# A hybrid recurrence and convolution layer: the launch's scheduler orders the instructions by its timeline model

## The chip, the cores and the metric

The kernel runs on one core of one Trainium2 chip. The metric is the device time of one execution in microseconds (us); a value given for a kernel is the median over its runs. A profile is one further execution that the hardware profiler recorded, with a time of its own. The engines are PE (matrix products; PEld is its weight load), DVE (vector), ACT (scalar and activations), POOL, and SP, which here only issues DMA.

## The reference

One layer over a sequence of 2048 tokens of width 1024, with a context of 256 tokens:

```
shift, scale, gate = split(silu(c) @ w_ada + b_ada, 3)      # the same with c_ctx for the context
h  = rmsnorm(x, norm_w) * (1 + scale) + shift
p  = h @ w_in                                               # 1024 x 9216
q, v, zf, zb = four of the five column groups of p, 8 heads of 128 each
f  = lb + (1 - lb) * sigmoid(z)                             # forward and backward; k = 1 - f
S_t = diag(f_t) S_{t-1} + k_t v_t^T ;  o_t = S_t^T q_t      # in both directions, started from the context's states
y_hg = rmsnorm(o) * silu(gate columns)
y_cv = b * conv3(c * h) * silu(gate)                        # within rows of 64 tokens, four more column groups
out  = rmsnorm(x + gate * (concat(y_hg, y_cv) @ w_out), final_norm_w)
```

All is float32 in the reference.

## The kernel before, in words

**Products.** A float32 operand is split into two float16 parts, and each product takes three matmuls (high by high, high by low, low by high; lines 839 to 841). On top of that the input and the output projection use a seven-product scheme for 2x2 blocks (`seven`, from line 830) instead of eight, for which sums and differences of blocks of weights and tokens are formed first. These operands are named B11, T1, T2, B21, T3, B22, T4 on the token side; they are prepared once per group of 512 tokens and stored in DRAM (Hd).

**Stages in the program.** (1) The start, lines 1238 to 1264: the first 512 tokens (x, four tiles of 128x1024) are loaded, squared on ACT (L220) and normalised on DVE (L225); a pair of weight tiles is loaded (L333, `load_pair`); then `modulate` (from L177) loads the modulation matrix in sixteen tiles `wa` of 512 KB (L182) into four buffers (the tags f and K, two each) and multiplies it (`pada`, L184), with the transposes of the first tokens and a second pair of weights between its steps. Only after `modulate` does the program load the context's two tiles (`xt_c`) and the second token group's four tiles (printed as `x` in the profile) at L1259. The context's tiles use the tag Q of six buffers, the second group's four tiles are set aside in the pool `hp`. `modulate_end` and `affine` make scale and shift of `pada`, and the first products follow (`plain`, L1346 to L1348). (2) Eight heads in four segments of 512 tokens each, 32 windows: in each, the products for gates, values and queries of one segment go beside the scan of the segment before (`scan_steps`, L636). The scan is a chain: a diagonal product (`Ad`, L528), five levels (`A`, L554) in each of which PE multiplies, DVE updates K and Q (L414, L421), ACT copies (`km`, L537), then two more levels (L568, L578), the transposes of K, the states (L602) and the output (`o`, L658 and L659). The tiles f and K that carry it have two buffers. (3) Short convolutions, 18 windows. At their first, pools are closed and others opened, and large operands C are loaded back (L900). (4) The output projection, from about 1800 us of the profile on.

**What sets the order of the work.** Two things. First the program: in each window, `run` (L1294) emits the products, and between them, by weights in a table PACE (L45), the steps of the scan and of other preparations. Second the launcher's scheduler. When the tile context of line 1520 is closed, it walks the traced program in a simulated machine: an engine (or SP, which issues DMA) that is free there gets the earliest instruction of the program whose inputs are finished, and whose buffer has come free, at that simulated moment. So an instruction can be passed by later ones. The order that comes out is fixed; semaphores are then put in for it, and on the chip each engine takes its instructions strictly in that order and waits where one isn't ready. Which physical buffer a tile gets is set in the same walk.

The context's constructor has a switch for the simulated machine. Without it, the scheduler uses its default model of what instructions and transfers take.

## Time and profile before

| | us |
|---|---|
| median of 3 runs | 2226.85 |
| lowest and highest | 2223.29, 2228.72 |
| the profiled execution, its own time | 2224.16 |
| its span from first to last instruction | 2222.2 |

| engine | busy us | share of the span |
|---|---|---|
| PE | 2113.2 | 95% |
| DVE | 1659.9 | 75% |
| ACT | 1158.3 | 52% |
| POOL | 112.5 | 5% |

In the profile, `out<-in` names the tile written and the tiles read, `x8` counts instructions in a row or a group, and `[0.20 <-DMA wa]` at the end of a row says that the engine had been idle for 0.20 us and what ended this. In the table of windows each row is a stretch of the span: its length, then the busy time of PE, PEld, DVE, ACT and POOL with the number of instructions in parentheses, the granted PE clock (1.00 is full), the mean busy share of the 16 DMA engines, and GB/s. In the groups, the figures behind the bar are busy us and mean ns of one, then idle time before them. In a table of waits they are us in total, number of times, and the longest. SPq marks SP's queue: the rows of it are issues of DMA, not the transfers.

### The profile page before, as it was taken

What the parts mean: (1) busy time and instruction counts of PE and PEld (TensorE: products, weight loads), DVE (VectorE), ACT (ScalarE), POOL (GpSimd) and SP (SyncE); (2) the same over time, 40 slices, a digit from 0 to 9 for tenths busy, and PEclk for the clock granted to TensorE, in tenths of its full rate; (3) what the DMA queues carried; (4) which work ended last, traced back from release to release, by engine and by line L of the source; (5) the groups of instructions that cost most, each with busy time, mean ns of one, the idle gap of its engine ahead of it and who ended that gap; (6) DMA issues with size and microseconds to landing.
All of it is one profiled execution on the core that took longest, in us unless ns stands there. A gap on an engine that the chain in (4) does not pass through costs nothing.

```text
span 2222.2 us, 51962 instructions
## 1 busy us (share of the span) xinstructions
PE 2113.2 (95%) x21563; PEld 1466.6 (66%) x21563; DVE 1659.9 (75%) x3515; ACT 1158.3 (52%) x2313; POOL 112.5 (5%) x207
## 2 busy tenths in 40 slices
PE   4889899999999999999999999999999999999998
PEld 1767688888888888888888887444444444444443
DVE  6987877968779778788687786587678646677775
ACT  6655655665567555666676554354445313333332
POOL 0211100000000000000000000000000000000000
PEclk8889999999999999999999999999999999999999
DMA  8664343433243333333543357842343224633321
GB/s 324 223 212 169 103 137 103 153 95 117 82 158 112 106 120 119 108 111 122 191 134 131 126 183 248 240 137 101 108 138 116 68 90 157 232 106 122 120 99 57
DMA packets 191040, 309.89 MB, mean 139 GB/s; under 512 B 13138, under 2 KB 123090, under 8 KB 189012
## 3 DMA queue, kind: packets, MB, share of 16 engines
q1 hardware_dynamic: 188644, 302.64, 41.5%
q8 instruction: 169, 2.77, 0.5%
q10 hardware_dynamic: 2160, 3.93, 0.5%
q14 instruction: 67, 0.55, 0.1%
HBM read 241.50 MB, written 65.01 MB: 138 GB/s over the span
## 4 chain that ended last, share of the span: by engine, by line
PE 66%; DVE 15%; DMA 7%; ACT 6%; issue 4%; SPq 1%; POOL 1%; POOLq 0%; DVEq 0%; ACTq 0%
PE sa L839 8%; PE sa L841 7%; PE sa L840 7%; PE sb L839 4%; PE sb L840 3%; PE sb L841 3%; DMA ws_p<-in_w_in 3%; PE sa_o L839 2%; PE sa_o L841 2%; PE sa_o L840 2%; PE A L554 2%; PE T L602 2%; PE sc L839 2%; PE sc L841 2%; PE sc L840 2%
## 5 line engine op out<-in xcount | busy, mean ns | idle before, releaser
L840 PEld LDWEIGHTS <-e_p 128*128 128x128 f16 x1368 | 134.8, 99 | 66.8 <-issue 17.1
L414 DVE TENSOR_TENSOR K<-K,tot 128x512 f32<-128x512 f32 x192 | 132.0, 688 | 61.8 <-PE A L578 24.6
L839 PEld LDWEIGHTS <-e_p 128*128 128x128 f16 x1368 | 134.5, 98 | 60.2 <-issue 3.3
L841 PEld LDWEIGHTS <-e_p 128*128 128x128 f16 x1368 | 134.8, 99 | 53.1 <-issue 0.8
L421 DVE TENSOR_TENSOR Q<-Q,tot 128x512 f32<-128x512 f32 x192 | 132.6, 691 | 33.3 <-PE A L554 32.9
L537 ACT ACTIVATE km<-K 128x512 f32<-128x512 f32 x160 | 109.1, 686 | 86.3 <-DVE K L414 60.6
L840 PEld LDWEIGHTS <-whib_p 128*128 128x128 f16 x912 | 89.2, 98 | 45.5 <-issue 13.3
L586 POOL COPY A<-Ac 32x128 f32<-32x128 f32 x128 | 66.4, 519 | 1007.1 <-ACT A L582 649.2
L839 PEld LDWEIGHTS <-whib_p 128*128 128x128 f16 x912 | 89.1, 98 | 40.8 <-issue 3.7
L840 PEld LDWEIGHTS <-whia_p 128*128 128x128 f16 x912 | 89.3, 98 | 37.9 <-issue 6.3
L839 PEld LDWEIGHTS <-whia_p 128*128 128x128 f16 x912 | 89.2, 98 | 37.5 <-issue 0.8
L841 PEld LDWEIGHTS <-wloa_p 128*128 128x128 f16 x912 | 89.3, 98 | 34.3
L841 PEld LDWEIGHTS <-wlob_p 128*128 128x128 f16 x912 | 89.2, 98 | 34.3
L151 ACT ACTIVATE e_p<-ws_p,sc_p 128x512 f16<-128x512 f32 x108 | 77.2, 716 | 61.4 <-DVE ws_p L376 39.4
L341 ACT ACTIVATE junk<-ws_p 128x1024 f16<-128x1024 f32 x72 | 76.0, 1055 | 55.7 <-DMA ws_p<-in_w_in 55.2
L846 ACT ACTIVATE u<-sa,sx_w 128x256 f32<-128x256 f32 (+1 forms) x114 | 59.8, 524 | 70.9 <-PE sa L841 56.1
L554 PE MATMUL A<-Q,km 128*32 128x32 f32 x5120 | 77.9, 202 | 12.4 <-DVE Q L421 6.4
L554 PEld LDWEIGHTS A<-Q,km 128*32 128x32 f32 x5120 | 58.9, 112 | 46.4 <-issue 20.3
L762 ACT ACTIVATE cv<-c,small 128x512 f32<-128x512 f32 (+1 forms) x36 | 24.2, 671 | 109.2 <-DVE c L780 48.9
L152 DVE SCALAR_TENSOR_TENSOR e_p<-ws_p,sc_p,e_p 128x512 f16<-128x512 f32 x108 | 78.0, 743 | 2.5 <-ACT e_p L151 2.4
L846 ACT ACTIVATE p<-sb,sx_w 128x256 f32<-128x256 f32 (+1 forms) x114 | 59.3, 520 | 35.6 <-PE sb L841 34.0
L846 ACT ACTIVATE p<-sa,sx_w 128x256 f32<-128x256 f32 (+1 forms) x114 | 58.8, 516 | 32.2 <-PE sa L841 32.1
(865 smaller groups left out, 6881.7 us busy)
## 6 DMA issues: line engine op xcount, KB each, us to landing
ws_p<-in_w_in SPq DMA_DIRECT2D x72, 512.0 KB, 4.4
y_o<-yT SPq DMA_DIRECT2D x32, 512.0 KB, 3.8
wa<-in_w_ada SPq DMA_DIRECT2D x16, 512.0 KB, 5.4
Gd<-zs SPq DMA_DIRECT2D x32, 256.0 KB, 3.5
sg<-Gd SPq DMA_DIRECT2D x32, 256.0 KB, 4.1
yT<-y SPq DMA_DIRECT2D x32, 256.0 KB, 2.3
wos_a<-in_w_out SPq DMA_DIRECT2D x16, 512.0 KB, 4.6
yT<-sg SPq DMA_DIRECT2D x64, 128.0 KB, 2.6
```

The lines of the kernel that those rows point to most:

```text
L151: S.activation(hi, src, AF.Copy, scale=st[:, 0:1])
L152: V.scalar_tensor_tensor(lo, src, st[:, 0:1], hi, ALU.mult, ALU.subtract)
L341: S.activation(junk.rearrange("p (k n) -> p k n", k=KT), stage[i], AF.Abs, accum_out=r)
L414: V.tensor_tensor(m, m, sub(cur, nb + 1, [[2, np_], [-(nb + 1), 2], [0, B]]), ALU.mult)
L421: V.tensor_tensor(m, m, sub(cur, 1, [[2, np_], [nb - 1, 2], [0, B]]), ALU.mult)
L537: S.activation(sub(s.km, 0, [[2 * B, n // (2 * B)], [B, 2], [1, B]]), mix(s.K, n, B, n // (2 * B)), AF.Copy)
L554: PE.matmul(pt[j * SB:(j + 1) * SB, ch * SB:(ch + 1) * SB], s.km[:, o:o + SB], mix(s.qf, n, B, SB // (2 * B), o), start=True, stop=True)
L586: G.tensor_copy(A3[js, :, js], s.Ac[js])
L839: PE.matmul(ps, hi[:, k], rh, start=start and k == 0, stop=False, skip_group_check=not start)
L840: PE.matmul(ps, hi[:, k], right(name, 1, k), start=False, stop=False, skip_group_check=not start)
L841: PE.matmul(ps, lo[:, k], rh, start=False, stop=k == nk - 1, skip_group_check=not start)
L846: S.activation(r, ps, AF.Copy, scale=sx)
```

## The change

One argument of the tile context in the launch; the traced program is the same.

```
-    with tile.TileContext(nc) as tc:
+    with tile.TileContext(nc, schedule_with_timeline_sim=True) as tc:
         hybrid_layer(tc, *args)
```

With it, the scheduler walks the program on its timeline model, another simulation of the same machine with other prices for instructions, for the issue of DMA and for transfers. No instruction is added or removed; what can differ is the order on PE, DVE, ACT, POOL and in SP's queue, which buffer a tile gets, and the semaphore waits that follow from both.

## Prediction

> **What bounds the kernel now.** I read the page's first block, then the table of windows (the span cut by stage), then the two ends of the kernel in the timeline, and last what the tensor engine (PE) waits for. The first block:
>
> ```profile
> span 2222.2 us, 51962 instructions
> PE 2113.2 (95%) x21563; PEld 1466.6 (66%) x21563; DVE 1659.9 (75%) x3515; ACT 1158.3 (52%) x2313; POOL 112.5 (5%) x207
> ```
>
> PE has a record open for 2113.2 of 2222.2 us, so it is idle for 109 us. The change alters no instruction, only the order in which each engine and each DMA queue takes them. It can win at most what PE idles, and it can lose without such a limit. The windows show where the idle time lies (length of the stretch, then busy time by engine, granted PE clock, DMA share, GB/s):
>
> ```profile
> 0.00:50.00 50.00, 24.07 (x106) 7.74 (x107) 29.09 (x81) 29.92 (x49) 0.83 (x5) 0.92 0.87 319
> 50.00:150.00 100.00, 78.84 (x778) 63.49 (x776) 89.73 (x252) 69.23 (x140) 26.59 (x47) 0.83 0.72 232
> 150.00:300.00 150.00, 133.68 (x1769) 113.39 (x1769) 119.65 (x268) 77.11 (x151) 23.37 (x40) 0.98 0.45 143
> 300.00:1200.00 900.00, 887.80 (x12919) 765.87 (x12917) 704.20 (x1577) 565.26 (x1260) 50.01 (x96) 1.00 0.37 120
> 1200.00:1350.00 150.00, 147.24 (x1994) 128.40 (x1992) 114.41 (x267) 92.10 (x224) 7.53 (x16) 1.00 0.58 184
> 1350.00:1440.00 90.00, 81.58 (x502) 48.64 (x500) 53.64 (x105) 30.23 (x51) 0.00 (x0) 1.00 0.79 239
> 1440.00:1800.00 360.00, 348.29 (x1600) 152.74 (x1598) 259.21 (x429) 156.69 (x243) 0.00 (x0) 1.00 0.34 114
> 1800.00:2100.00 300.00, 299.75 (x1390) 135.80 (x1389) 209.23 (x362) 101.72 (x142) 0.00 (x0) 1.00 0.40 134
> 2100.00:2222.00 122.00, 111.92 (x520) 50.50 (x518) 80.72 (x182) 36.05 (x56) 4.16 (x3) 0.98 0.26 87
> ```
>
> Length minus PE's busy time gives the idle time: 25.9, 21.2 and 16.3 us in the first three rows (63.4 us in 300 us), then 12.2, 2.8, 8.4 and 11.7 us (35.1 us in the next 1500), 0.3 us in the first part of the output projection and 10.1 us at the end. So there are three regimes: a start limited by DMA (share 0.87) and then by DVE (89.73 of 100 us) ahead of PE; a middle limited by PE; an end that nothing but PE limits.
>
> A record that is open isn't yet an array at work, so I also look at how the products start in the middle:
>
> ```profile
> 628.78 0.27 PE L839 MATMUL sa<-hop13T,whib_p 128*128 128x256 f16 x1
> 628.89 0.27 PE L840 MATMUL sa<-hop13T,whib_p 128*128 128x256 f16 x1
> 629.00 0.27 PE L841 MATMUL sa<-hop13T,wlob_p 128*128 128x256 f16 x1
> ```
>
> Records of 0.27 us start 0.11 us apart, evenly, whatever matrix they use: the stream is back to back, and an order can't make it denser.
>
> **The change, part by part.** The scheduler gives an engine that is free in its simulated machine the earliest instruction of the program whose inputs and buffers are ready there. Another machine gives another order only where the two disagree on what is ready. I take the stages one by one.
>
> *Start, 0 to 50 us.* SP's queue in the order of time, with what follows from it:
>
> ```profile
> 4.79 15.23 SPq L182 DMA_DIRECT2D wa<-in_w_ada  x8
> 20.07 4.65 SPq L333 DMA_DIRECT2D ws_p<-in_w_in  x2
> 24.81 10.87 SPq L182 DMA_DIRECT2D wa<-in_w_ada  x8
> 35.73 0.90 SPq L216 DMA_DIRECT2D xt_c<-in_ctx  x2
> 36.67 3.22 SPq L216 DMA_DIRECT2D x<-in_x  x4
> 42.57 1.92 PE L184 MATMUL pada<-wa,sc 128*32 128x512 f32 x4 [0.20 <-DMA wa<-in_w_ada]
> 43.85 1.06 ACT L220 ACTIVATE junk<-xt_c 128x1024 f16<-128x1024 f32 x1 [6.00 <-DMA xt_c<-in_ctx]
> 49.43 0.37 PE L1346 MATMUL u<-hop0B,whia_p 128*128 128x256 f16 x1 [1.68 <-ACT hop0B L265]
> ```
>
> This is the program's own order, unaltered: all sixteen modulation tiles (wa) go before the context (xt_c) and the second token group (x). Yet those loads need no buffer that is in use: the Q tag has six buffers, of which the first group takes four, and x1's four tiles are set aside in the hop pool. The default model therefore must have thought SP occupied all the time. On the chip it wasn't: six loads take 0.90 + 3.22 = 4.12 us to issue, about 0.7 us each, while the first eight wa loads spread over 15.23 us, because each waits for one of four buffers. A model nearer to that would find SP free between them, and would put the third weight tile (0.5 MB), the two context tiles (1.0 MB) and x1's four (2.0 MB) into that time. That is the edit that I expect to matter: 3.5 MB move from after the modulation into it.
>
> What it costs or brings on the path to the first product goes by how full DMA is:
>
> ```profile
> 10.00:15.00 5.00, 1.09 (x7) 0.44 (x9) 3.51 (x16) 3.41 (x6) 0.00 (x0) 1.00 1.03 416
> 15.00:20.00 5.00, 4.60 (x26) 1.84 (x20) 4.20 (x9) 2.96 (x5) 0.00 (x0) 1.00 0.74 264
> 50.00:55.00 5.00, 1.61 (x8) 0.96 (x7) 5.00 (x11) 4.46 (x9) 3.84 (x7) 0.50 1.01 382
> 60.00:70.00 10.00, 10.00 (x91) 8.69 (x90) 9.67 (x29) 7.25 (x15) 3.33 (x6) 1.00 0.89 362
> ```
>
> By 50 us, 319 GB/s x 50 us = 16 MB have arrived. At the 416 GB/s of the first row here that is 38 us, so a queue that never runs empty would be some 8 us ahead with everything after its first 3 to 4 us. Against it, 3.5 MB in front of the third pair of wa tiles hold them up by 3.5 / 0.416 = 8.4 us if none of it falls into idle time. The last modulation product (42.57 us) thus moves between -8 and +8.4 us. I take -2: the empty time (share 0.74 just there) is about as large as the insertion, and the wa tiles still turn round in four buffers.
>
> *What is relieved afterwards, 50 to 150 us.* With context and x1 in place by then, their squares on ACT and their normalisation on DVE can run while the modulation still loads. DVE is the engine that PE waits for here. In the groups of 44 to 80 us:
>
> ```profile
> L225 DVE TENSOR_SCALAR x<-x,rsy_x 128x1024 f32<-128x1024 f32 x4 | 3.2, 822 | 0.0
> L225 DVE TENSOR_SCALAR xt_c<-xt_c,rsy_c 128x1024 f32<-128x1024 f32 x2 | 1.4, 748 | 0.0
> L129 DVE SCALAR_TENSOR_TENSOR rsa_c<-rsy_c 128x2 f32<-128x2 f32 x3 | 0.5, 161 | 0.0
> ```
>
> 3.2 + 1.4 us, and two reciprocal roots of 11 small operations of 0.16 us each (3.5 us), make 8.1 us of DVE that leave the crowded stretch for one with 29.09 of 50 us. PE is full from 60 to 70 us (10.00 of 10), so not all of it arrives; bounds 0 and -8.1, and I take -5, nearer to the full relief since DVE is at 90%.
>
> *150 to 300 us.* The third and fourth token groups are normalised and turned here; 16.3 us of PE idle time, at most half of which I give to order (bounds 0 and -8). I take -3.
>
> *Middle, 300 to 1800 us.* What PE waits for over the whole run:
>
> ```profile
> PE ss_p L139 <- DVE rb_p L345: 15.2, 4, 13.9
> PE pada L184 <- DMA wa<-in_w_ada: 7.6, 8, 2.4
> PE A L554 <- DVE Q L421: 6.4, 8, 2.2
> PE xT_x L232 <- DVE xt_x L225: 5.3, 2, 4.9
> ```
>
> Three of the four longest belong to the start. The level products (A, L554), which the scan depends on at 160 places, waited 8 times, 6.4 us in all. Little is left to win: as one bound the 8.4 us of 1350 to 1440 us, where the pools change and large loads stand on SP; as the other, one wait of their mean, 6.4 / 8 = 0.8 us, in each of the 32 segments, +26 us. I take 0, nearest to the 12.2 us of idle time in 900.
>
> *Output projection and end.* 0.3 us of idle time in 300, and its last matmuls keep program order whatever is simulated; 0, within 1 us.
>
> The sum: -2 - 5 - 3 + 0 + 0 = -10 us on the profiled execution's own 2224.16 us, so 2214.2. It lies 2.7 us under the median of the three runs shown (2226.85), so the prediction in terms of that median is **2217 us**, 0.44% faster. About 0.3%, 6.7 us, is what a measurement of this kernel can tell from no change.
>
> **Rivals.**
>
> *No change (2227 us, between 2220 and 2233).* The priority of program order makes the new order nearly the old one, or the relief is eaten up: PE is already full between 60 and 70 us, and whatever comes earlier may only wait there. That the flag does nothing is in it too. For it: through the middle PE has no gap that another order could fill, and there every model finds the same instruction first in line.
>
> *Slower at the start (2235 us).* The same seven loads go in front, none of their 8.4 us falls into idle time, and no relief arrives: 2226.9 + 8.4. It decides at the last modulation product: if it starts after some 47 us instead of 42.57, the loads displaced what PE needed first.
>
> *Slower in the middle (2253 us).* The machine that has the engines' latencies differently puts the steps of a segment's scan further back among the products. Two rows of the groups for 560 to 720 us, and one of the timeline, give the room:
>
> ```profile
> L528 PE MATMUL Ad<-q,ks x128: 196/196/217, 598.3 to 697.2; 128*32 128x32 f32 x128
> L658 PE MATMUL o<-v,A x32: 275/275/275, 582.9 to 693.9; 128*128 128x128 f32 x32
> 625.03 0.39 PE L658 MATMUL o<-v,A 128*128 128x128 f32 x2
> ```
>
> Four segments end between 582.9 and 693.9 us, 37 us apart; one begins at 598.3 and ends at 625.03, a chain of 27 us. So 10 us of slack stand between the scan and the products. A scan that slips by under 10 us costs nothing; once some ten steps slip by over 1 us each, the two buffers of f and K are not free for the next gates and PE stops. Priced at the 0.8 us a segment from above, +26 us. Against it: the slack, and that the present waits are tiny.
>
> *The clock comes along (2204 us).* The granted clock follows the gaps: 0.50 where PE works 1.61 of 5 us, 1.00 where it works 10.00 of 10, 0.83 over 50 to 150 us. If half clock and full clock are all there is, 0.83 is a third of that time at half clock, (1 - 0.83) / 0.5; a third of 78.84 us of work at half speed would shrink by half of it, 13 us. A start whose gaps close would win these besides: 2217 - 13. The Trainium skill, "TensorE: Matmul & The Clock Gate", section "What's actually happening", says that the array falls to half clock after an idle window of about 3.4 us and comes back after a busy one; the rows above agree with the two states. By that rule the same mechanism also punishes a start with longer gaps. Against this rival: gaps as short as those left in 80 to 140 us need only be rearranged, not closed, to keep the clock where it is.
>
> **How the numbers follow.** The forecast has 0.36, the clock 0.08, no change 0.25, slower at the start 0.16, slower in the middle 0.15. So faster by over 0.3%: 0.44; within 0.3%: 0.25; slower: 0.31. The forecast's own range is 2207 to 2223. Cases of both signs hold much of the chance, so the range for 8 in 10 reaches from 2203, which leaves out about half of the clock's case, to 2248, which takes in the slower start and a middle with most of its price: **2203 to 2248 us**.
>
> **What would show it.** Right: in the changed profile, the context and x1 loads stand on SP ahead of the third pair of wa tiles; ACT squares the context before 35 us; the last modulation product starts at 38 to 45 us; PE's idle time in 50 to 150 us falls from 21 to about 16 us, with 300 to 1200 us still at 10 to 15 us idle. Wrong: SP keeps the present order at the start (then the first term has no cause); the last modulation product comes after 47 us; or PE's idle time between 300 and 1800 us grows from 35 us to 50 or more, above all in front of L554 or of the products that write f and K.

## The result, and the profile after

| | before, us | after, us |
|---|---|---|
| median (4 runs each, measured together) | 2226.10 | 2260.74 |
| lowest and highest | 2223.29, 2228.72 | 2259.73, 2262.01 |
| span of the profiled execution | 2222.2 | 2259.5 |

The kernel became slower: the ratio is 1.0156, with a 95% interval of 1.0139 to 1.0174. The prediction was 2217 us, within 2203 to 2248. The first block of the page, and the same windows as in the prediction:

```profile
span 2259.5 us, 51890 instructions
PE 2121.4 (94%) x21563; PEld 1482.9 (66%) x21563; DVE 1641.4 (73%) x3515; ACT 1158.9 (51%) x2313; POOL 124.0 (5%) x207
```

```profile
0.00:50.00 50.00, 24.99 (x98) 7.12 (x98) 30.83 (x87) 36.05 (x60) 0.20 (x4) 0.80 0.98 389
50.00:150.00 100.00, 72.49 (x745) 61.05 (x744) 88.98 (x249) 63.64 (x128) 28.85 (x48) 0.82 0.54 179
150.00:300.00 150.00, 131.58 (x1768) 112.77 (x1767) 114.13 (x256) 76.02 (x148) 25.34 (x40) 0.97 0.47 147
300.00:1200.00 900.00, 865.29 (x12508) 749.85 (x12506) 672.01 (x1520) 547.78 (x1215) 55.14 (x92) 1.00 0.36 119
1200.00:1350.00 150.00, 144.71 (x2105) 125.61 (x2104) 113.54 (x259) 87.49 (x198) 10.03 (x19) 1.00 0.43 145
1350.00:1440.00 90.00, 83.77 (x657) 67.98 (x655) 57.11 (x146) 41.43 (x107) 0.65 (x2) 0.93 0.68 209
1440.00:1800.00 360.00, 351.78 (x1621) 158.71 (x1620) 257.98 (x429) 158.60 (x245) 0.00 (x0) 0.99 0.41 130
```

The instructions are the same 21563 matmuls. The row of 300 to 1200 us stands out: 34.7 us idle, against 12.2 before. Windows of fixed times no longer hold the same work once a kernel has slipped, though. So I cut both traces by work: every kernel here has 3640 records of L841 (the low-order part of a product), and a stretch runs from the start of its n-th record to the start of a later one. Length and PE's idle time, in us (the last column is taken before rounding):

| stretch, by records of L841 | before (idle) | after (idle) | longer by |
|---|---|---|---|
| span's start to the 1st | 104.3 (37.9) | 107.1 (38.7) | 2.8 |
| 1st to 274th | 174.3 (25.5) | 176.3 (32.3) | 2.0 |
| **274th to 1,730th, five and a quarter heads** | **773.7 (9.5)** | **801.7 (32.8)** | **27.9** |
| 1,730th to 2,185th, the last heads | 237.0 (4.6) | 237.4 (5.0) | 0.3 |
| 2,185th to 3,004th, pools change, convolutions | 505.8 (21.0) | 509.0 (16.7) | 3.2 |
| 3,004th to PE's last | 416.7 (0.3) | 416.7 (1.4) | 0.0 |

With 1.1 us behind PE's last record these are the 37.3 us by which the spans differ. The start, from which I expected the gain, lost 4.8 us; the middle, for which I had put down nothing, lost 27.9 in this stretch alone.

**The start.** SP's queue, then two rows of PE (timeline of after):

```profile
4.70 3.46 SPq L182 DMA_DIRECT2D wa<-in_w_ada  x4
9.47 1.40 SPq L216 DMA_DIRECT2D xt_c<-in_ctx  x2
15.49 3.23 SPq L182 DMA_DIRECT2D wa<-in_w_ada  x2
18.77 1.85 SPq L216 DMA_DIRECT2D x<-in_x  x4
...
27.34 5.89 SPq L182 DMA_DIRECT2D wa<-in_w_ada  x4
35.02 1.75 SPq L216 DMA_DIRECT2D xt_x<-in_x  x4
37.52 2.60 SPq L182 DMA_DIRECT2D wa<-in_w_ada  x4
...
48.64 1.47 PE L184 MATMUL pada<-wa,sc 128*32 128x512 f32 x6
...
59.35 1.15 PE L232 MATMUL xT_c<-ident,xt_c 128*128 128x128 f32 x4 [4.01 <-ACT h_c L250]
60.29 0.42 PE L1346 MATMUL u<-hop0B,whia_p 128*128 128x256 f16 x1
```

The order is the one that I expected, context and second group ahead of the third pair of wa tiles, and the third group's tiles (`xt_x`) ahead of the last four besides. The first plain product starts at 60.29 us instead of 49.43, 10.9 us later; by the first L841 record 2.8 of these are left. Part of the delay stands on DVE, whose work for later token groups now comes ahead of the scale and shift (`ab`) that the first products need (after):

```profile
56.36 2.07 DVE L225 TENSOR_SCALAR xt_x<-xt_x,rsy_x 128x1024 f32<-128x1024 f32 x3
58.41 0.23 DVE L206 TENSOR_SCALAR ab<-ab,sc_h 128x16 f32<-128x16 f32 x1
```

From the start of the last modulation product (49.52 us) to the start of the last `ab` it is 8.9 us; before it was 4.8 (43.43 to 48.26 us).

**The middle.** What PE waits for from 310 to 1090 us (after), in all, times, longest:

```profile
PE kT L593 <- DVE K L414: 7.5, 12, 0.8
PE sb L839 <- ACT p L846: 7.2, 5, 1.4
PE sa L839 <- DVE vT L850: 3.6, 4, 1.5
PE A L554 <- ACT Ac L530: 3.3, 4, 0.8
PE T L602 <- DVE y L742: 2.8, 3, 0.9
PE u L1332 <- ACT f L471: 2.3, 1, 2.3
```

No wait is longer than 2.3 us here; most of them recur once or twice per head. To see what they have in common I added up, over the long stretch, the time from the start of each PE record to the start of the next, by the kind of the two. Products following products: 490.5 us before, 491.0 after. Instructions of one scan line following each other: 164.6 and 164.2. A scan step following a product: 55.1 and 42.0; a product following a scan step: 37.5 and 49.7. And a scan step that directly follows another scan step of a different line (L658 and L659, which alternate, left out): 35 times in 6.0 us before, **140 times in 37.6 us** after, +31.6 us. Twenty of the 140 take over 0.5 us, 21.0 us together. The 31.6 us aren't a net cost, since steps behind a product became fewer: -13.1 us there, +12.2 where a product follows a step, and smaller differences give the 27.9. PE's idle time says where it stops: of the 32.8 us after, 17.6 stand ahead of a scan step directly behind another (0.3 before) and 14.9 ahead of a product directly behind a scan step (1.0 before). One such place, after, and the same place of the program before (timelines of PE):

```profile
744.23 0.27 PE L841 MATMUL sa<-hop15T,e_p 128*128 128x256 f16 x1
744.44 0.69 PE L578 MATMUL A<-Q,K 128*64 128x64 f32 x16
745.91 0.87 PE L593 MATMUL kT<-ident,K 128*128 128x128 f32 x6 [0.79 <-DVE K L414]
```

```profile
721.52 0.69 PE L578 MATMUL A<-Q,K 128*64 128x64 f32 x16
722.14 0.28 PE L839 MATMUL sc<-hop15B,whia_p 128*128 128x256 f16 x1
...
724.12 0.38 PE L593 MATMUL kT<-ident,K 128*128 128x128 f32 x2
```

Between the last level (L578) and the transposes of K (L593), DVE updates K (0.69 us). Before, 18 products stand between the two steps and hide that. After, none do; 26 products stand behind the transposes, and PE, which takes its queue in order, waits. The Trainium skill, "PSUM — Partial Sum Buffer", section "Engine vs sequencer instructions", says that matmuls start and complete in program order; the trace agrees, none of the 26 passed the waiting step in those 0.79 us.

The second row of the waits is of another kind. ACT and one row of PE, after:

```profile
540.50 1.14 ACT L151 ACTIVATE whia_p<-ws_p,sc_p 128x1024 f16<-128x1024 f32 x1
541.54 0.71 ACT L151 ACTIVATE whib_p<-s_p,sc_p 128x512 f16<-128x512 f32 x1
542.15 0.71 ACT L151 ACTIVATE whib_p<-ws_p,sc_p 128x512 f16<-128x512 f32 x1
542.76 0.71 ACT L151 ACTIVATE e_p<-ws_p,sc_p 128x512 f16<-128x512 f32 x1
543.38 0.62 ACT L453 ACTIVATE K<-f 128x512 f32<-128x512 f32 x1
543.89 0.46 ACT L846 ACTIVATE p<-sb,sx_w 128x256 f32<-128x256 f32 x1
...
544.40 0.27 PE L839 MATMUL sb<-hop11B,e_p 128*128 128x256 f16 x1 [1.43 <-ACT p L846]
```

PE wants the bank `sb` back, ACT reads it out with `p<-sb` (an evacuation, as I call such a read of a finished PSUM bank), and five bulk operations stand ahead of it on ACT.

### The profile page after: what moved, and what is told of

Same layout as the page of the kernel before. It is cut to its first block, busy times and chain, and to the rows that moved or that the text cites. A ratio compares the mean times of both kernels' runs of the same rounds, so it can differ in the third digit from the quotient of the medians.

```text
span 2259.5 us, 51890 instructions
## 1 busy us (share of the span) xinstructions
PE 2121.4 (94%) x21563; PEld 1482.9 (66%) x21563; DVE 1641.4 (73%) x3515; ACT 1158.9 (51%) x2313; POOL 124.0 (5%) x207
## 4 chain that ended last, share of the span: by engine, by line
PE 72%; DVE 8%; ACT 5%; DMA 4%; issue 3%; SPq 1%; POOL 0%; POOLq 0%; DVEq 0%; ACTq 0%
PE sa L839 9%; PE sa L841 9%; PE sa L840 9%; PE sb L839 4%; PE sb L840 4%; PE sb L841 4%; PE sa_o L839 2%; PE sa_o L840 2%; PE sa_o L841 2%; PE T L602 2%; PE A L554 2%; PE sc L839 2%; PE sc L841 2%; PE sc L840 2%; DMA ws_p<-in_w_in 2%
## 5 line engine op out<-in xcount | busy, mean ns | idle before, releaser
L841 PEld LDWEIGHTS <-e_p 128*128 128x128 f16 x1368 | 134.7, 98 | 53.2 <-issue 1.0
L586 POOL COPY A<-Ac 32x128 f32<-32x128 f32 x128 | 74.6, 583 | 1033.7 <-ACT A L582 730.1
L840 PEld LDWEIGHTS <-whib_p 128*128 128x128 f16 x912 | 89.4, 98 | 37.9 <-issue 5.2
L841 PEld LDWEIGHTS <-wloa_p 128*128 128x128 f16 x912 | 89.8, 98 | 35.8 <-issue 0.2
L841 PEld LDWEIGHTS <-wlob_p 128*128 128x128 f16 x912 | 89.4, 98 | 35.0 <-issue 1.1
L554 PE MATMUL A<-Q,km 128*32 128x32 f32 x5120 | 89.0, 203 | 19.5 <-DVE Q L421 10.5
L554 PEld LDWEIGHTS A<-Q,km 128*32 128x32 f32 x5120 | 65.0, 112 | 57.2 <-issue 32.7
L151 ACT ACTIVATE hiS_o<-y_o,sc_y 128x1024 f16<-128x1024 f32 x32 | 36.7, 1146 | 65.3 <-PE sa_o L840 26.6
```

Of the source, the lines that this page charges most:

```text
L151: S.activation(hi, src, AF.Copy, scale=st[:, 0:1])
L554: PE.matmul(pt[j * SB:(j + 1) * SB, ch * SB:(ch + 1) * SB], s.km[:, o:o + SB], mix(s.qf, n, B, SB // (2 * B), o), start=True, stop=True)
L586: G.tensor_copy(A3[js, :, js], s.Ac[js])
L840: PE.matmul(ps, hi[:, k], right(name, 1, k), start=False, stop=False, skip_group_check=not start)
L841: PE.matmul(ps, lo[:, k], rh, start=False, stop=k == nk - 1, skip_group_check=not start)
```

## The experiments

The theories in the expectations: A, PE's new order costs; B, the order on DVE and ACT does; C, the order of DMA and the buffers; D, neither is bad alone, but they must belong together. E to I were formed on the way. "The stretch" is the long one of the table: 773.7 us long and 9.5 idle before, 801.7 and 32.8 after.

### One engine in the program's own order (e1, e2)

```
+def in_order(tc, engines):                    # called behind hybrid_layer(tc, *args)
+    prev = {}
+    for ins in list(tc.nc.cur_bb.bb.instructions):
+        if ins.engine in engines:
...
+            tc.add_manual_dep(ins, prev[ins.engine], <issue order only>)
+            prev[ins.engine] = ins.name
+in_order(tc, (PE,))                # e1, on the changed kernel
+in_order(tc, (DVE, ACT, POOL))     # e2, on the changed kernel
```

> The changed kernel, with PE's instructions alone chained in the program's own order; DVE, ACT, GpSimd and the DMA queues still go by the timeline model. Theory A (PE's order is the cause: steps of a segment's scan are passed by products and by the next segment's levels, then bunch up): the 5 us per head go away, the heads take 147 to 148 us each again, PE idles 35 to 45 us between 300 and 1800, and the whole is 2225 to 2235 us, of which some 3 us are the start. Theory B (the order on DVE and ACT is the cause, which evacuates PSUM banks late): nothing of the 5 us per head goes, 2250 to 2265 us. Theory C (DMA order and buffers): 2250 to 2265 as well.

> The changed kernel, with DVE, ACT and GpSimd chained in the program's own order; PE and the DMA queues go by the timeline model. Theory A: PE is still out of order, 2250 to 2265 us, heads of 151 to 153 us. Theory B: 2225 to 2240 us, heads of 147 to 149 us. Theory C: 2250 to 2265.

e1: 2277.87 us; the stretch 792.1 us, 27.6 idle. e2: 2669.34 us, 139.0 us idle in the stretch. Neither was expected. In e1 direct successions fell back to 32 (35 before), and the stretch won 9.6 us of its 27.9, but the 32 take 18.6 us: among them are transposes that wait directly behind another step (L740 for ACT's kT, 8.6 us in five waits), and outside the stretch e1 takes 27 us more than the changed kernel (16.5 up to the 274th record, 10.6 in the last heads). The program's own order isn't the order of before, so e1 and e2 are weak on A and B. What e2 does show is how much the choice of an order is worth here: some 400 us.

### The start by itself (e3, e4)

```
+# e3, on the changed kernel: SP's first loads queued in the order of before
+for n, ins in enumerate(sp[1:], 1):
+    tc.add_manual_dep(ins, sp[min(n, 42) - 1].name, <issue order only>)
 # e4, on the kernel before
+    ctx_norm = norm_group(2, cx, 0, 1, "c")
     def between(k):
         first[4][k][1]()
-        if k == VQ_AT:
+        if k == 1:
             next_w(0)
+            for _, st in ctx_norm[0]: st()
+        if k == 2:
+            for _, st in x1_norm[0]: st()
```

> The changed kernel, with the 32 loads at the start chained on SP in the order of before (all sixteen modulation tiles ahead of the context and of the second token group); everything behind them goes by the timeline model. My reading of the two traces: the last modulation product is back at 43 to 45 us and the first plain product at 49 to 53 us (60.3 in the changed kernel), but the relief on DVE is gone too, so only about 3 us are won by 200 us, and the whole is 2255 to 2260. Rival (the start's 11 us last to the end): 2248 to 2251.

> The kernel before, default model, with one edit by hand: the third weight tile, the two context tiles and the second token group's four tiles are loaded after the second and the third pair of modulation tiles, as the changed kernel has them, in place of after the last pair. My reading: the first plain product comes 6 to 11 us later (49.4 before), 3 us are left of it by 200 us, the whole is 2228 to 2231. The forecast on record had this edit at -7 us (2 at the modulation, 5 of relief): 2219 to 2221. Rival (the 11 us last): 2236 to 2239.

e3: 2257.58 us, as I expected, and 3.2 us less than the changed kernel, which isn't clear of noise (ratio to the kernel before 1.0136, 1.0120 to 1.0153, against 1.0156, 1.0139 to 1.0174); the last modulation product and the first plain product came 1.2 and 1.9 us earlier than before, and the stretch stayed slow (805.5 us). e4: 2227.23 us, ratio 1.0003 (0.9994 to 1.0013), just under my 2228 to 2231 and far from the 2219 to 2221 of the forecast. So what I forecast as the gain is worth nothing. Where it went can be seen in e4: the last modulation product comes 7.2 us later, yet the third group's transposes start at 94.19 us instead of 101.38, so the relief is real. Then the first product on hop1B starts at 106.92 instead of 103.52, after PE has waited 3.92 us for its load. Its operand goes through DRAM, by stores and loads that SP issues; first store and first load, before and then e4:

```profile
76.42 0.60 SPq L268 DMA_DIRECT2D Hd1B<-hpB_x  x1
...
99.35 0.57 SPq L1231 DMA_DIRECT2D hop1B<-Hd1B  x1
```

```profile
81.58 0.60 SPq L268 DMA_DIRECT2D Hd1B<-hpB_x  x1
...
102.64 0.55 SPq L1231 DMA_DIRECT2D hop1B<-Hd1B  x1
```

That chain starts 5.2 us later and its first load is issued 3.3 us later; it follows the late modulation, and the relieved products run into it.

### Engines in exactly the order of before (e5 to e9)

```
+order = [<names of engine e's instructions, in the order of the scheduled block of before>
+         for e in ENGINES]       # the program is built first with the default model
+nc = program(order, schedule_with_timeline_sim=True)   # each name queued behind the one ahead of it
+ENGINES = (PE,)                  # e5
+ENGINES = (DVE, ACT, POOL)       # e6
+ENGINES = (PE, ACT)              # e7
+ENGINES = (PE, DVE)              # e8
+ENGINES = (PE, DVE, ACT, POOL)   # e9: only SP's queue is left to the timeline model
```

> The changed kernel, with PE's instructions in exactly the order of the kernel before (its program is built first, and PE's order is taken from it); DVE, ACT, GpSimd and the DMA queues go by the timeline model. Theory A (PE's order is the cause; the program's own order, 2277.87 us, was merely a still worse one): 2225 to 2235 us, heads of 147 to 148 us. Theory B (the order of DVE and ACT is the cause): 2245 to 2265 us, heads of 150 to 153 us. Theory D (neither order is bad alone, but PE's and the evacuating engines' must belong together): 2240 to 2275 us.

> The changed kernel, with DVE, ACT and GpSimd in exactly the order of the kernel before; PE and the DMA queues go by the timeline model (its order still breaks off from the one of before 1,720 times, against 1,717 in the changed kernel). Theory A: 2250 to 2265 us. Theory B: 2225 to 2240 us. Theory D: 2240 to 2275 us, so that this run and the one with PE as before are both slow.

> The changed kernel, with PE and ACT in exactly the order of the kernel before; DVE, GpSimd and the DMA queues go by the timeline model. If ACT's order is what delays (the page of the changed kernel shows a 1.4 us wait per head for an evacuation that ACT took three conversions later than before): 2226 to 2232 us. If it is DVE's: no better than with PE alone as before, 2245 to 2265 under theory B. Under theory A it is 2225 to 2235 like the run with PE alone.

> The changed kernel, with PE and DVE in exactly the order of the kernel before; ACT, GpSimd and the DMA queues go by the timeline model. If DVE's order is what delays (kT from DVE's K is the changed kernel's longest wait of PE in the heads, 7.5 us): 2226 to 2232 us. If it is ACT's: 2245 to 2265 under theory B. Under theory A 2225 to 2235.

> The changed kernel, with PE, DVE, ACT and GpSimd in exactly the order of the kernel before; only the DMA issues on SP go by the timeline model. Theory E (formed from the runs with one or two engines as before: every computing engine's new order costs by itself, 4 to 6 us per head, and the costs do not add; the DMA order costs only at the start and where the pools change): heads of 147 to 148 us, 8 to 9 us lost by the first products and not relieved, some 10 us lost in front of the products that read hop34B, and 2236 to 2250 us in all. Rival (theory C: DMA order and buffers make the heads slow): heads of 150 us and more, 2260 to 2300 us.

| | us | stretch, us | idle in it |
|---|---|---|---|
| e5, PE as before | 2294.81 | 800.7 | 29.3 |
| e6, DVE, ACT, POOL as before | 2323.65 | 817.0 | 43.9 |
| e7, PE and ACT as before | 2302.08 | 796.0 | 28.4 |
| e8, PE and DVE as before | 2293.96 | 801.0 | 30.6 |
| e9, all but SP as before | 2250.39 | 773.9 | 10.0 |

e9 settles C for the heads: with PE, DVE, ACT and POOL as before, and the DMA order and the buffers from the timeline model, the stretch is back to 773.9 us. The loss there is one of the order on the computing engines. The whole, 2250.39 us, is 0.4 us over the range of E. e5 to e8 are all slower than any theory had them (2275 us at most). A and B fall as far as they name one engine: neither PE's old order nor that of the others wins the loss back. (30.3 of e7's 75 us are one wait for ACT's u, in front of the first convolutions; its heads are like the others'.)

How a single engine left to the timeline model stops the rest can be read in the traces. In e8 ACT runs ten output scalings (L734) ahead of an evacuation, and six more ahead of the next; the kernel before has rows of six and of one to four there, with the evacuations in between:

```profile
498.76 3.01 ACT L734 ACTIVATE Q<-Q,rsy_o 128x128 f32<-128x128 f32 x10
501.68 0.57 ACT L661 ACTIVATE Q<-o 128x512 f32<-128x512 f32 x1
502.16 1.85 ACT L734 ACTIVATE Q<-Q,rsy_o 128x128 f32<-128x128 f32 x6
...
504.44 0.46 ACT L846 ACTIVATE p<-sa,sx_w 128x256 f32<-128x256 f32 x1
```

PE feels it at one remove: DVE waits 4.02 and 1.59 us for ACT's `zs` (L712), which stands behind the scalings, updates Q late, and a level product (L554) waits 1.83 us for Q at 508.60 us.

In e7 ACT has its old order, but DVE makes one weight sum (L373) later, and all that stands behind it on ACT waits, an evacuation (f_c) among it, and PE for that:

```profile
741.32 0.72 ACT L151 ACTIVATE e_p<-ws_p,sc_p 128x512 f16<-128x512 f32 x1 [3.46 <-DVE ws_p L373]
...
743.65 0.33 PE L839 MATMUL sa<-hop15B,whia_p 128*128 128x256 f16 x1 [3.42 <-ACT f_c L457]
```

e9 also shows the price of the DMA order by itself, 21.5 us on the profiled spans. By stretches: 5.1 up to the 274th record (with PE and DVE in their old order the earlier loads relieve nothing), 0.2 in the heads, 16.8 from the 2,185th to the 3,004th record. The largest piece of the last: twelve loads of C (four before) stand ahead of four loads of hop34 that the last products of the heads' stage need. SP before, then e9, then what PE waits for in e9:

```profile
1331.91 0.33 SPq L1231 DMA_DIRECT2D hop34B<-Hd2B  x1
...
1342.38 2.21 SPq L900 DMA_DIRECT2D C0B<-Hd0B  x1
```

```profile
1342.53 3.77 SPq L900 DMA_DIRECT2D C0T<-Hd0T  x1
...
1349.87 1.68 SPq L900 DMA_DIRECT2D C0B<-Hd1B  x1
1351.64 1.61 SPq L1231 DMA_DIRECT2D hop34B<-Hd2B  x1
```

```profile
PE sc L839 <- DMA hop34B<-Hd2B: 10.2, 1, 10.2
```

The changed kernel has the same order (hop34B at 1385.12 us, behind twelve C loads from 1364.03 on), but its own computing order gives the loss back in the convolutions: 3.2 us are left of 16.8.

### One suspected cost in the kernel before, and the mixed orders (e10 to e12)

```
+# e10, before: all engines in their own order, but on ACT each head's 16 scalings at the place of the first
+names[:] = rest[:at] + sorted(row, key=names.index) + rest[at:]
+# e11, default model: PE in the order of the changed kernel
+# e12, default model: DVE, ACT and POOL in the order of the changed kernel
```

> The kernel before, default model, with PE, DVE and GpSimd in its own order and ACT in its own order but for one thing: the 16 output scalings of a head stand in one row at the place of the first (before: rows of 1 to 8 with evacuations of PSUM banks in between). 16 x 0.30 us is 4.8 us of ACT ahead of every evacuation that was in between. If bulk work ahead of evacuations is what stops PE (theory E for ACT): 1 to 3 us per head that PE waits for ACT's evacuations, 2235 to 2250 us. Rival (ACT, busy 63% of the time in the heads, catches up unnoticed): 2224 to 2231 us.

> The kernel before, default model, with PE alone in exactly the order of the changed kernel; the default model orders DVE, ACT, GpSimd and the DMA issues around it. Stretch of measure: PE's idle time in the 3,640 products of the hop stage from the 274th to the 1,730th (273.7 to 1052 us before), 9.5 us before, 32.8 in the changed kernel, 10.0 with only the DMA order new. Theory E (PE's new order costs by itself): 25 to 35 us idle there, 2240 to 2270 us in all. Rival (PE's new order is harmless if the default model chooses what DVE and ACT do next to it): 9 to 15 us idle there, 2225 to 2240 us.

> The kernel before, default model, with DVE, ACT and GpSimd in exactly the order of the changed kernel; the default model orders PE and the DMA issues around them. Theory E (what the timeline model does on DVE and ACT costs by itself): 25 to 45 us of PE's idle time in the same stretch, 2240 to 2290 us in all. Rival (only PE's order next to it makes it costly): 9 to 15 us idle there, 2225 to 2240 us.

e10: 2233.89 us, ratio 1.0031 (1.0018 to 1.0043). In most heads PE waits some 0.7 us more once, where a level product (L554) waits for DVE's Q, and 2.9 us more at the first, for ACT's q. The time lies between the two ranges, and 0.7 us is less than the 1 to 3 of E. So bulk work in a row on ACT does stop PE, in the heads by way of DVE as in e8, but the scalings alone are a small part of 5 us a head. e11: 2334.51 us, 68.5 us idle in the stretch; e12: 2441.95 us, 74.1 idle. Both are worse than the whole change and than all that was expected, and E can't be right as it stood ("every engine's new order costs 4 to 6 us a head by itself"). In these runs an order made on one model cost most when the rest was arranged around it by the other. That is theory D, with one consequence for e5 to e8: they can't be read as shares of single engines.

### How far ahead, and what ahead of what (e13 to e18)

```
+for first, later in zip(row, row[24:]):       # row: one engine's instructions as traced; DVE and ACT
+    tc.add_manual_dep(later, first.name, <issue order only>)
+# e13: on the changed kernel.  e14: and PE as in e1.  e15: on the kernel before
+# e16 to e18, on the changed kernel: a weight split is queued behind the last such instruction ahead of it
+#   e16: evacuation p5 (p from sb), ACT.  e17: any evacuation, ACT and DVE.  e18: anything, ACT and DVE
```

> The changed kernel, with a limit of 24 places on how far DVE and ACT may run ahead in the program (each instruction is queued behind the one 24 places before it on its engine); PE and the DMA issues go freely by the timeline model. Stretch of measure: PE's idle time between the 274th and the 1,730th record of the low-order products (L841), 9.5 us before and 32.8 in the changed kernel. Theory F (DVE and ACT run too far ahead, so that bulk work stands in front of evacuations): 12 to 22 us idle there, 2235 to 2250 us in all. Rival G (PE's own run-ahead is what costs, or how the orders fit together): 28 to 40 us idle there, 2255 to 2275 us.

> The same with PE's instructions also chained in the program's own order (that chain alone, without the limit: 27.6 us idle in the stretch, 2277.87 us). Theory F: 10 to 18 us idle there, 2245 to 2262 us in all, since the chain on PE costs some 20 us more than before outside the heads. Rival G, if PE's run-ahead is what costs: also under 18 us there, while the run without the chain stays over 28. If neither holds: 25 us or more in both.

> Control: the kernel before, default model, with the same limit of 24 places on DVE and ACT (a tenth of their instructions stand further ahead in the kernel before: 22 places on DVE and 19 on ACT is the 90th percentile). If the limit costs nothing by itself: 9 to 14 us idle in the stretch, 2224 to 2235 us. If it costs: 20 us idle and more, 2240 us and more, and then a slow run with the limit on the timeline model says nothing against theory F.

> The changed kernel with one rule on ACT: a weight split (L151) is queued behind the evacuation of the second bank (p from sb) that stands before it in the program. 4 splits pass such an evacuation instead of 58. Stretch as in the runs before: 32.8 us of PE's idle time in the changed kernel. Theory H (such waits simply add up, and each can be taken away): the 7.2 us of waits for p from sb fall under 2, 25 to 28 us idle in the stretch, 8 heads x 1.4 = 11 us in all, 2248 to 2254 us. Rival I (another wait takes the place): 31 to 36 us idle, 2257 to 2267 us.

> The changed kernel with a wider rule on ACT and DVE: a weight split (L151, L152) is queued behind every evacuation of a PSUM bank that stands before it in the program on its engine. Theory H: another 3 to 6 us less than with the narrow rule (the 3.6 us of waits for vT and 1.7 us for z on DVE are of this kind), 20 to 25 us idle in the stretch, 2243 to 2250 us. Rival I: 31 to 38 us idle, 2257 to 2270 us.

> The changed kernel with the widest rule: a weight split is queued behind every other instruction that stands before it in the program on its engine (ACT, DVE). This takes in the 7.5 us for which PE waits for DVE's K (L414, 12 waits), if splits are what stands in front there. Theory H: 14 to 22 us idle in the stretch, 2236 to 2246 us. Rival I: 31 us and more; if splits that come too late are a cost of their own, as with the limit of 24 places, 40 us and more and 2265 to 2290 us.

| | us | stretch, us | idle in it |
|---|---|---|---|
| e13, limit, timeline model | 2291.52 | 826.8 | 45.0 |
| e14, limit, PE in program order | 2279.69 | 797.4 | 34.1 |
| e15, limit, default model | 2248.54 | 785.9 | 21.9 |
| e16, splits behind p5 | 2262.99 | 802.3 | 27.2 |
| e17, splits behind evacuations | 2262.18 | 797.9 | 24.7 |
| e18, splits stay put | 2277.18 | 805.8 | 30.2 |

F gets no support, but isn't refuted. With and without the chain on PE idle time stays over 25 us, so neither F's numbers came nor G's for PE. But the control shows that the limit costs by itself, and by what was put down for that case the slowness of e13 then says nothing against F. What speaks against it is that the limit doesn't bring the models closer: it costs 12.4 us of idle time on the default model (e15) and 12.2 on the timeline model (e13), so that their distance stays at 23, and by length the distance grows from 27.9 to 40.9 us. A gain from less running ahead could still hide behind a dearer limit.

e16 is the instructive one. The wait for `p` from `sb`, 7.2 us, is gone from the list altogether, and the idle time fell by 5.6 us, as H said. The stretch is no shorter: 802.3 against 801.7 us. PE's busy time in it rose from 768.9 to 775.1 us. Two things took the place. Other waits came or grew: steps next to the small product of the weights' scale (L139) take 8.2 instead of 2.5 us, 5.1 of them waits of the states (L602) for DVE's y, and one product waits 2.8 us for ACT's f_c. And the granted clock fell, right behind that wait (windows of 4 us, e16):

```profile
1036.00:1040.00 4.00, 1.25 (x41) 0.96 (x40) 3.18 (x5) 3.87 (x7) 0.00 (x0) 1.00 0.74 258
1040.00:1044.00 4.00, 4.00 (x38) 2.84 (x39) 2.10 (x5) 2.79 (x6) 0.00 (x0) 0.60 0.17 29
```

At the granted clock of 0.50 products start 0.21 us apart instead of 0.11. The stretch has 6.8 us of this, here and at 331 us, with PE busy in 6.5; half of that, some 3 us, is an estimate of what it cost. The changed kernel's stretch has none. So the result is I in time, and H in idle time; without the slow clock, by this estimate, some 3 us of the gain would be left. e17 won 3.8 us of the stretch and lost them elsewhere, e18 lost. In all three, direct successions of scan steps stay (152, 138 and 142 times, 34.5 to 37.8 us), and `kT <- K` keeps its twelve waits and 7.6 us.

None of these kernels is faster than the one before; e4 equals it.

## Why the prediction was wrong

*The step that failed:* "I take 0, nearest to the 12.2 us of idle time in 900" for the middle, bounds -8.4 and +26. It measured +27.9 in five and a quarter heads alone, over the upper bound. The argument that stands with it, under the rival "no change" ("there every model finds the same instruction first in line"), is what the trace contradicts: direct successions of scan steps went from 35 to 140. PE being busy 98.6% of 300 to 1200 us said that the order of before hid every step of the scan; it didn't say that another order would.

*The rival "slower in the middle"* had the place and nearly the size (26 us) and got 0.15. Its mechanism was half right. I priced a scan that slips back as a whole, argued 10 us of slack for it, and looked for PE stopping at the products that write f and K. The only such wait in the heads is 2.3 us, once. What the traces show instead needs no slip: the products were dealt out unevenly. Rows of 26 and more between two steps came 91 times instead of 42 in the stretch, and none between two steps 140 times instead of 35. As I read it, slack over a whole segment doesn't help then, since what hides a step is the work that stands directly behind it.

*The start's order* came as forecast: which loads, and ahead of which. *The last modulation product* was put at -2 and measured +6.1 (+7.2 in e4): most of the insertion of 8.4 us did not fall into empty time, and the upper bound was nearer than the middle. *A term was missing:* another 4.8 us up to the first plain product. PE now does most of the context's transposes first and waits 4.01 us for ACT's h_c, but 4.1 of the 4.8 us are the longer way to `ab` on DVE shown above, where normalisations of the second and third token groups (L225) now stand in between. *The relief* was put at -5 of at most -8.1, and 10.9 - 2.8 = 8.1 us were made up by the first L841 record. That it equals the bound is luck, since ten of the context's sixteen transposes, which used to come behind that product, are part of it. *150 to 300 us:* -3 forecast; from the 1st to the 274th record +2.0. All in all -10 forecast, +4.8 measured, and +0.3 at the 274th record where the start is changed alone (e4). *The pool change and convolutions* had been part of the middle's bound: +3.2 net. *The output projection:* 0 forecast, 0.0 measured.

*The clock* gave nothing and was lower in places: granted 0.80 and 0.82 in the first two windows, 0.92 and 0.83 before, and 0.93 from 1350 to 1440 us, 1.00 before. In the long stretch it was full in both kernels. One window of after, at the start:

```profile
55.00:60.00 5.00, 0.88 (x5) 0.53 (x5) 5.00 (x19) 1.26 (x4) 0.82 (x2) 0.50 0.01 3
```

The Trainium skill, "TensorE: Matmul & The Clock Gate", section "What's actually happening", has the array at half clock after an idle window of about 3.4 us. The trace agrees in so far as the clock is 0.50 across the 4.01 us gap of this window; it had fallen before that gap, though (0.75 from 50 to 55 us), so this gap didn't start it.

*What would show it wrong* was named and came: the last modulation product after 47 us (its group of rows starts at 48.64), and PE's idle time between 300 and 1800 us over 50 us. By the rows of after it is 34.7 + 5.3 + 6.2 + 8.2 = 54.4 us. From 50 to 150 us PE idled 27.5 us, where 16 was to show the forecast right.

*Shown and not shown.* Shown: the loss in the heads is the order on the computing engines (e9), not the loads (e3, e9). Spoken against, but not excluded: that it is how far DVE and ACT run ahead (e13, e15). Taking out one repeated wait on ACT won no time (e16 to e18), in e16 partly because the clock fell. Read in the traces only: that PE stops at scan steps directly behind scan steps (17.6 of the 32.8 us idle) and at products directly behind them (14.9). A run that pulls products between just those steps, with all else as in the changed kernel, wasn't made; e1, which brought their number back to 32 by another order of PE, won 9.6 us of the stretch and lost more elsewhere. What in the timeline model leads to that order stays open.

## What to carry to other kernels

When a change leaves all instructions and alters only their order, an engine that is 98% busy has little to win and, as here, much to lose: count, for each step of a dependent chain, how much independent work stands directly behind it on its engine, and ask what a less even dealing would cost. An order is one piece: a half of it taken from another schedule cost up to 215 us here, more than either whole. And measure such edits by the length of a stretch of equal work, not by idle time or by one wait, which can vanish without a gain, and read the granted clock of that stretch beside it.

## What the runs showed of the hardware

PE's busy time isn't fixed by its instructions. In the long stretch, at full granted clock in all three, PE was busy 764.3 us before, 768.9 after and 773.0 in e6: part of the waiting lies inside records that are open. In e6 a product that waits for ACT's p starts 1.71 us after the one ahead of it, 0.11 without a wait, and 1.44 of this counts as idle, so 0.16 us of the loss doesn't. An idle time alone understates a loss. The clock adds to it: over the whole run the same 21563 matmuls took 2113.2 us of busy time before and 2188.9 in e12, but there PE was busy at half the granted clock for 135.6 us instead of 36.6, and half of the difference, an estimate of its price, is 49.5 of the 75.7 us. And an issue of DMA can be dear: of the C loads in e9, 512 KB each and close on one another, the first three took SP 0.59, 0.66 and 0.99 us to issue and most of those behind them about 1.7 us, so that twelve ahead of hop34B held SP's queue from 1330.54 to 1351.64 us.
